# Sample attention with a chunk-free unit at every third turn, and two sets of operands prepared in the same units

## The chip, the cores and the metric

The kernel runs on one core of a Trainium2 chip. The time is that of one execution on the device, in microseconds (us); lower is better. A second, profiled execution of the same program gives the trace.

## What is computed

One layer of a decoder trunk, for a prompt of 512 tokens and for 8 samples of 4 new tokens each (544 columns in all, d_model 2048), float32 throughout:

```
h    = rmsnorm(x) * g_pre
proj = h @ w_in                       # pu, pz, q, kv, ag, az, su, sz, mg
br_pool = (pool_mixer(pu)         * silu(pz)) @ w_br_pool
br_att  = (sparse_attention(q,kv) * silu(az)) @ w_br_nsa
z       = gelu(s5(su))
br_ssm  = (z * sigmoid(z @ w_glu) * silu(sz)) @ w_br_ssm
merged  = sum over branches of sigmoid(mg) * br
y       = x + rmsnorm(merged @ w_out) * g_post
```

The samples attend to 2048 cached positions each, which lie in pages that a page table names: a compressed copy of them, the selected blocks of them, and a window of 512.

## The kernel before

**Units.** TensorE (PE) gets almost all of its work as *units*: a tile of weights of 128 x 1024 numbers against 544 columns. Each float32 matrix is split in a high and a low part of a rounded type, and `mm3` (L154 to L156) multiplies high x high, low x high and high x low. A unit of the input projection (`in_unit`) is 48 such matmuls of 272 columns; a pool unit is 24. There are 218 input units and 4 pool units, then 8 GLU units, 48 branch units, 32 output units. The weights of a unit come by one DMA of 512 KB (`w_load`, L138) into one of three buffers `wr`; ScalarE makes `whi` (L149) and VectorE `wlo` (L150).

**Background work.** Everything else (cache compression, the state-space scan, both attentions, the operands of the next stage) is written as Python generators. `step(u, ...)` emits one unit: it runs what was deferred, lets each generator in `bg` go on to its next `yield`, evicts the unit before (L332, on VectorE), and emits the unit's matmuls. So the number of yields decides beside which unit a piece of background work stands, and each engine works its instructions off in the order in which they were emitted. `main_bg` chains the generators: `g_compress`, `g_ssm`, `g_compress_prompt`, `g_prompt`, `g_decode`, `prep_y(0, ...)`, `prep_z`. With the flag `early` (it is on in `g_compress`, `g_ssm`, `g_decode` and the two preparations) the weights of the unit after next are split and the next load is issued ahead of the background work.

**Compression.** `g_compress` has 16 jobs (8 samples, two halves of a block). A job needs 16 pages of 128 KB, which SyncE's queue (SP) gathers into a tile `ca` of two buffers (L604). A job is three pieces of 20, 20 and 24 matmuls (L638), one unit apart; the gathers for the next job go out with the first and second piece.

**Decode.** `g_decode` walks 20 chunks (4 pairs of samples, 4 chunks of selected positions and one window chunk). Two generators alternate inside it: `s_gen` makes the scores of a chunk from the key tiles `gk` (L1478) and asks for the `gk` two chunks ahead; `p_gen` transposes the weights (L1529), multiplies the chunk before with the value tiles `gv` (L1561) and asks for the `gv` two chunks ahead. Each pass of the loop `while gens` is one turn, and there is one `yield`, so one unit, per turn:

```
        while gens:
            for g in gens[:]:
                try:
                    next(g)
                except StopIteration:
                    gens.remove(g)
            yield
```

`gk` and `gv` have four buffers each, two per chunk. A chunk's gathers are 8 DMAs of 128 KB for `gk` and 8 for `gv`; a window chunk has two DMAs of 512 KB in place of the eight (`wkT`, `wv`). In front of every four gathers SP reads page numbers (`TENSOR_LOAD ptrow`).

**Operands.** `prep_y(0, ...)` loads the pool branch and its gate (`ly`, `lz`), multiplies them (L1628), and splits the product in `yhA` (ScalarE, L1606) and `ylA` (VectorE, L1610), one tile of 128 x 544 per unit. `prep_z` then loads the scan's output in `ly` (L1652, L1654), makes its gelu (square L1644, scale L1645, product L1646, tanh L1647, product L1640), and splits it in `yhB`, `ylB`. The eight GLU units that follow use `yhB`, `ylB`; the first branch uses `yhA`, `ylA`. PSUM has three buffers `d` for the units' sums.

Of the kernel before, what the change touches and what calls it, by code (L numbers as in the profile page):

```python
# [10 lines left out]
F32 = mybir.dt.float32  # L11
F32R = mybir.dt.float32r
I32 = mybir.dt.int32
AF = mybir.ActivationFunctionType
OP = mybir.AluOpType
# [8 lines left out]
TOK = TP + NB * TS  # L24
# [42 lines left out]
def kernel(ctx, tc, a):  # L67
    nc = tc.nc
    pe, dve, act, pool, sp = nc.tensor, nc.vector, nc.scalar, nc.gpsimd, nc.sync
# [25 lines left out]
    ypool = drt("ypool", [8, 128, TOK])  # L95
# [511 lines left out]
    def g_compress():  # L607
        with ExitStack() as s:
            cp = s.enter_context(R("cmp"))
            wphi = cp.tile([128, 2, 32, 64], F32, name="wphi")  # L610
            sp.dma_start(wphi, a["wphi"])
            ca_s = ExitStack()
            cap = ca_s.enter_context(R("ca", 2))
            jobs = [(b, h) for b in range(8) for h in range(2)]
            tiles = {}

            def fetch(n, pages):
                if n >= len(jobs):
                    return
                b, h = jobs[n]  # L620
                if n not in tiles:
                    tiles[n] = cap.tile([128, 16, 256], F32, name="ca")
                gather([tiles[n][:, pg, :] for pg in pages], f"c{h}", b * 16 + pages[0])
            for pg in range(0, 16, 4):
                fetch(0, range(pg, pg + 4))
                yield
            acc_b = None
            for n, (b, h) in enumerate(jobs):
                t = tiles.pop(n).rearrange("q g (k e j) -> q g k e j", k=2, j=8)
                if h == 0:  # L630
                    acc_b = bank("s", 2)
                for d0, d1, pgs in ((0, 5, (0, 8)), (5, 10, (8, 16)), (10, 16, ())):
                    if pgs:
                        fetch(n + 1, range(*pgs))
                    for d in range(d0, d1):
                        dd = h * 16 + d
                        for k in range(2):
                            pe.matmul(acc_b[k * 64:(k + 1) * 64, :128], lhsT=wphi[:, k, dd, :],  # L638
                                      rhs=t[:, :, k, d, :], start=(dd == 0), stop=(dd == 31))
                    yield  # L640
                if h:
                    act.activation(KC[:, b, :], acc_b[:, :128], AF.Copy)
            yield
            ca_s.close()
        done.add("cache")
# [677 lines left out]
    def g_decode():  # L1323
# [239 lines left out]
            next_of(vpos, get_v)  # L1563

        gens = [p_gen(), s_gen()]
        while gens:
            for g in gens[:]:
                try:
                    next(g)
# [3 lines that stand above are left out]
# [20 lines left out]
    YH, YL = {}, {}  # L1593
# [20 lines left out]
    def prep_y(br, src, sil):  # L1614
        YH[br], YL[br] = [], []
        yz, fins = {}, []
        for k in range(10):
            if k < 8:
                y = yps["ld"].tile([128, TOK], F32, name="ly", bufs=3)
                z = yps["ld"].tile([128, TOK], F32, name="lz")  # L1620
                sp.dma_start(y, src[k])
                sp.dma_start(z, zsil[sil][k])
                yz[k] = (y, z)
            if fins:
                fins.pop()()
            if 0 < k < 9:
                y, z = yz.pop(k - 1)
                dve.tensor_tensor(y, y, z, op=OP.mult)  # L1628
                fins.append(split_y(br, y, 0.5))
            yield  # L1630

    def prep_z():
        YH["z"], YL["z"] = [], []
        yz, mid, fins = {}, [], []
        for k in range(11):
            if fins:
                fins.pop()()
            if mid:
                y, z = mid.pop()
                dve.scalar_tensor_tensor(y, z, 1.0, y, op0=OP.add, op1=OP.mult)  # L1640
                fins.append(split_y("z", y, 0.5))
            if 0 < k < 9:
                y, z = yz.pop(k - 1)
                act.activation(z, y, AF.Square)  # L1644
                dve.tensor_scalar(z, z, 0.044715, 1.0, op0=OP.mult, op1=OP.add)  # L1645
                dve.tensor_tensor(z, z, y, op=OP.mult)  # L1646
                act.activation(z, z, AF.Tanh, scale=0.7978845608028654)  # L1647
                mid.append((y, z))
            if k < 8:
                y = yps["ld"].tile([128, TOK], F32, name="ly", bufs=3)  # L1650
                z = yps["ld"].tile([128, TOK], F32, name="lz")
                sp.dma_start(y[:, :512].rearrange("q (l m) -> q l m", l=8),  # L1652
                             y_p[:, 2 * k:2 * k + 2].rearrange("l c g m -> (c g) l m"))
                sp.dma_start(y[:, 512:].rearrange("q (t b) -> q t b", t=4),  # L1654
                             y_s[:, 2 * k:2 * k + 2].rearrange("l c g b -> (c g) l b"))
                yz[k] = (y, z)
            yield


# [12 lines left out]
    def main_bg():  # L1672
        early[0] = True
        yield from g_compress()
        yield from g_ssm()
        early[0] = False
        yield from g_compress_prompt()
        yield from g_prompt()
        early[0] = True
        yield from g_decode()  # L1680
        att_s.close()
        open_y()
        yield from prep_y(0, ypool, "pz")
        yield from prep_z()

    first_tiles()
    u = 0
# [58 lines left out]
    def br_unit(u, b, m):  # L1746
# [10 lines left out]
        def evac():  # L1757
            g = gt.pop((b, m))
            if b == FIRST:
                o = acc_p.tile([128, TOK], F32, name="acc")  # L1760
            else:
                o = g
            for hf in range(2):
                c = slice(hf * HALF, (hf + 1) * HALF)
                dve.scalar_tensor_tensor(o[:, c], g[:, c], 1.0, ps2[hf][:, :HALF], op0=OP.add, op1=OP.mult)
            if b == FIRST:
                ACC[m] = o
            elif b != LAST:
                pool.tensor_tensor(ACC[m], ACC[m], o, op=OP.add)
            else:  # L1770
                dve.tensor_tensor(o, ACC.pop(m), o, op=OP.add)
                h = yps["B"].tile([128, TOK], F32R, name="mh", tag=("yhB", "ylB")[m // 8])
                l = acc_p.tile([128, TOK], F32R, name="ml", tag="acc")
                act.activation(h, o, AF.Copy, scale=0.5)
                dve.scalar_tensor_tensor(l, o, 0.5, h.bitcast(F32), op0=OP.mult, op1=OP.subtract)
                if m == 0:
                    MS.append(yps["ld"].tile([128, 16, 32], F32, name="lz"))
                act.activation(MS[0][:, m], o[:, TP:], AF.Copy, scale=0.5)
                MH[m], ML[m] = h, l
        step(u, mms, evac)  # L1780
# [400 lines left out]
```

## Time and profile before

| what | value |
|---|---|
| median of 3 runs | 2268.2 us (2267.27 to 2268.97) |
| the profiled execution's own time | 2266.38 us |
| its span, first to last instruction | 2264.5 us |
| mean granted TensorE clock | 0.997 |
| PE busy | 2238.5 us, 99% |
| weight loads of PE | 2110.6 us, 93% |
| VectorE, ScalarE, GpSimd busy | 1091.3, 643.9, 119.1 us |
| moved by DMA | 359.60 MB, 159 GB/s |

Read it so: the span is the time between the first and the last instruction of the profiled execution; 1.9 us of its own time lie around it. Matmuls are pipelined, and a matmul that the trace shows as 0.29 us long is followed by the next after 0.125 us; PE busy means that one was under way, not that it ran at its best pace. The granted clock is a share of 2.4 GHz; 0.50 is 1.2 GHz.

### The profile page before, as it was taken

What the parts mean: (1) busy time and instruction counts of PE and PEld (TensorE: products, weight loads), DVE (VectorE), ACT (ScalarE), POOL (GpSimd) and SP (SyncE); (2) the same over time, 40 slices, a digit from 0 to 9 for tenths busy, and PEclk for the clock granted to TensorE, in tenths of its full rate; (3) what the DMA queues carried; (4) which work ended last, traced back from release to release, by engine and by line L of the source; (5) the groups of instructions that cost most, each with busy time, mean ns of one, the idle gap of its engine ahead of it and who ended that gap; (6) DMA issues with size and microseconds to landing.
All of it is one profiled execution on the core that took longest, in us unless ns stands there. A gap on an engine that the chain in (4) does not pass through costs nothing.

```text
span 2264.5 us, 46954 instructions
## 1 busy us (share of the span) xinstructions
PE 2238.5 (99%) x19510; PEld 2110.6 (93%) x19510; DVE 1091.3 (48%) x1999; ACT 643.9 (28%) x1110; POOL 119.1 (5%) x101
## 2 busy tenths in 40 slices
PE   9999999999999999999999999999999999999998
PEld 8899999999999999999999998779999999998778
DVE  6334553347863236766666334332455536453224
ACT  5111111132122114445444323222343212222221
POOL 2000000230052000000000000000000002100000
PEclk9999999999999999999999999999999999999999
DMA  6767776643346765223222468884554645343334
GB/s 228 196 174 195 203 225 197 146 123 106 110 124 144 206 209 169 86 91 116 92 90 77 135 206 248 262 264 153 196 136 141 216 153 203 129 142 107 101 101 153
DMA packets 290791, 359.60 MB, mean 159 GB/s; under 512 B 136338, under 2 KB 210835, under 8 KB 289555
## 3 DMA queue, kind: packets, MB, share of 16 engines
q1 hardware_dynamic: 290578, 356.60, 51.7%
q8 instruction: 154, 2.52, 0.5%
q14 instruction: 59, 0.48, 0.1%
HBM read 310.69 MB, written 54.13 MB: 161 GB/s over the span
## 4 chain that ended last, share of the span: by engine, by line
PE 96%; DMA 2%; SPq 1%; DVE 0%; issue 0%; ACT 0%; ACTq 0%
PE d L154 25%; PE d L156 24%; PE d L155 24%; PE s L638 3%; PE o L1281 2%; PE s L1217 2%; PE t L1257 2%; PE d L1861 2%; PE d L1862 1%; PE d L1863 1%; PE t L1861 1%; PE s L999 1%; PE t L1862 1%; PE t L1863 1%; PE s L1478 1%; PE o L1561 1%
## 5 line engine op out<-in xcount | busy, mean ns | idle before, releaser
L154 PE MATMUL d<-xh,whi 128*128 128x272 f32 x3424 | 1008.0, 294 | 5.5 <-ACT xh L239 5.5
L156 PE MATMUL d<-xl,whi 128*128 128x272 f32 x3424 | 986.4, 288 | 0.0
L155 PE MATMUL d<-xh,wlo 128*128 128x272 f32 x3424 | 985.2, 288 | 0.0
L154 PEld LDWEIGHTS d<-xh,whi 128*128 128x128 f32 x3424 | 646.4, 189 | 31.4 <-issue 20.6
L156 PEld LDWEIGHTS d<-xl,whi 128*128 128x128 f32 x3424 | 646.3, 189 | 1.0 <-DVE xl L240 1.0
L155 PEld LDWEIGHTS d<-xh,wlo 128*128 128x128 f32 x3424 | 646.6, 189 | 0.0
L150 DVE TENSOR_TENSOR wlo<-wr,whi 128x1024 fp32r<-128x1024 f32 x297 | 377.2, 1272 | 510.3 <-ACT whi L149 488.3
L149 ACT ACTIVATE whi<-wr 128x1024 fp32r<-128x1024 f32 x297 | 311.6, 1052 | 739.9 <-PE d L156 485.5
L332 DVE TENSOR_TENSOR e<-d,rstd 128x272 f32<-128x272 f32 x186 | 81.5, 438 | 248.3 <-PE d L156 235.1
L154 PE MATMUL d<-yhA,whi 128*128 128x272 f32 x512 | 148.0, 289 | 0.0
L156 PE MATMUL d<-ylA,whi 128*128 128x272 f32 x512 | 147.7, 288 | 0.0
L155 PE MATMUL d<-yhA,wlo 128*128 128x272 f32 x512 | 147.3, 288 | 0.0
L156 PE MATMUL d<-ylB,whi 128*128 128x272 f32 (+2 forms) x384 | 110.8, 289 | 0.0
L154 PE MATMUL d<-yhB,whi 128*128 128x272 f32 (+2 forms) x384 | 110.8, 289 | 0.0
L155 PE MATMUL d<-yhB,wlo 128*128 128x272 f32 (+2 forms) x384 | 110.4, 287 | 0.0
L154 PEld LDWEIGHTS d<-yhA,whi 128*128 128x128 f32 x512 | 96.3, 188 | 0.0
L155 PEld LDWEIGHTS d<-yhA,wlo 128*128 128x128 f32 x512 | 96.3, 188 | 0.0
L156 PEld LDWEIGHTS d<-ylA,whi 128*128 128x128 f32 x512 | 96.2, 188 | 0.0
L1236 ACT ACTIVATE pt<-s,mm 128x512 f32<-128x512 f32 (+3 forms) x128 | 66.7, 530 | 36.8 <-DVE mm L1232 36.1
L638 PE MATMUL s<-ca,wphi 128*64 128x128 f32 x1024 | 67.6, 280 | 5.8 <-DMA ca<-c 5.8
L155 PEld LDWEIGHTS d<-yhB,wlo 128*128 128x128 f32 x384 | 72.3, 188 | 0.0
L154 PEld LDWEIGHTS d<-yhB,whi 128*128 128x128 f32 x384 | 72.2, 188 | 0.0
(428 smaller groups left out, 2531.2 us busy)
## 6 DMA issues: line engine op xcount, KB each, us to landing
wr<-wd SPq DMA_DIRECT2D x297, 512.0 KB, 3.8
ca<-c SPq DMA_DIRECT2D x256, 128.0 KB, 3.7
gk<-ck SPq DMA_DIRECT2D x128, 128.0 KB, 3.1
gv<-cv SPq DMA_DIRECT2D x128, 128.0 KB, 3.0
gates<-e SPq DMA_DIRECT2D x48, 272.0 KB, 3.9
lg<-gates SPq DMA_DIRECT2D x48, 272.0 KB, 4.0
wo<-wd SPq DMA_DIRECT2D x12, 512.0 KB, 3.5
wphi<-wphi SPq DMA_DIRECT2D x2, 2048.0 KB, 10.7
```

The source lines that it names most:

```text
L149: act.activation(hi, r, AF.Copy)
L150: lo_eng[0].tensor_tensor(lo, r, hi.bitcast(F32), op=OP.subtract)
L154: pe.matmul(ps, lhsT=h, rhs=xh, start=start, stop=False)
L155: pe.matmul(ps, lhsT=l, rhs=xh, start=False, stop=False)
L156: pe.matmul(ps, lhsT=h, rhs=xl, start=False, stop=stop)
L332: dve.tensor_tensor(out[:, cols(hf)], ps[:, :HALF], rstd[:, cols(hf)], op=OP.mult)
L638: pe.matmul(acc_b[k * 64:(k + 1) * 64, :128], lhsT=wphi[:, k, dd, :], rhs=t[:, :, k, d, :], start=(dd == 0), stop=(dd == 31))
L1217: pe.matmul(st[n][k][:, off:off + nk], lhsT=QS[pg][k][:, qt * 128:(qt + 1) * 128], rhs=KS[br, k][j][:, :nk], start=(j == 0), stop=(j == 1))
L1236: act.activation(pt[:, off:off + nk], b[:, off:off + nk], AF.Exp, scale=0.125, bias=m_[:, k, j:j + 1], accum_out=s_[:, k, j:j + 1])
L1257: pe.transpose(b[:, c:c + 128], st[n][k][:, c:c + 128], ident)
L1281: pe.matmul(o[hs[k], qt * 128:(qt + 1) * 128], lhsT=VN[:, kb, br, pg // 4, hs[k]], rhs=st[n][k][:, off + kb * 128:off + (kb + 1) * 128], s ...
L1861: pe.matmul(ps[:, :w], lhsT=MH[k][:, c], rhs=h[:, j], start=(k == 0), stop=False)
```

## The change

```
@@ g_compress
             for pg in range(0, 16, 4):
                 fetch(0, range(pg, pg + 4))
                 yield
+            yield
             acc_b = None
@@ g_decode
         gens = [p_gen(), s_gen()]
+        turn = 0
         while gens:
+            turn += 1
+            if turn > 3 and turn % 3 == 1:
+                yield
             for g in gens[:]:
@@ prep_y
-                z = yps["ld"].tile([128, TOK], F32, name="lz")
+                z = yps["ld"].tile([128, TOK], F32, name="lz", bufs=3)
@@ prep_z becomes prep_first
-    def prep_z():
-        YH["z"], YL["z"] = [], []
-        yz, mid, fins = {}, [], []
+    def prep_first():
+        for br in (0, "z"):
+            YH[br], YL[br] = [], []
+        ld, mid_, fin0 = {}, [], []
         for k in range(11):
-            if fins:
-                fins.pop()()
-            if mid:
-                y, z = mid.pop()
+            if fin0:
+                fin0.pop()()
+            finz = None
+            if mid_:
+                y, z = mid_.pop()
                 dve.scalar_tensor_tensor(y, z, 1.0, y, op0=OP.add, op1=OP.mult)
-                fins.append(split_y("z", y, 0.5))
-            if 0 < k < 9:
-                y, z = yz.pop(k - 1)
-                act.activation(z, y, AF.Square)
-                dve.tensor_scalar(z, z, 0.044715, 1.0, op0=OP.mult, op1=OP.add)
-                dve.tensor_tensor(z, z, y, op=OP.mult)
+                finz = split_y("z", y, 0.5)
+            now = ld.pop(k - 1, None)
+            if now:
+                y0, z, y = now
+                dve.tensor_tensor(y0, y0, z, op=OP.mult)
+                fin0.append(split_y(0, y0, 0.5))
+                act.activation(z, y, AF.Square, scale=0.21146071)
+            if finz:
+                finz()
+            if now:
+                dve.scalar_tensor_tensor(z, z, 1.0, y, op0=OP.add, op1=OP.mult)
                 act.activation(z, z, AF.Tanh, scale=0.7978845608028654)
-                mid.append((y, z))
+                mid_.append((y, z))
             if k < 8:
-                y = yps["ld"].tile([128, TOK], F32, name="ly", bufs=3)
-                z = yps["ld"].tile([128, TOK], F32, name="lz")
+                y0, z, y = (yps["ld"].tile([128, TOK], F32, name=n, bufs=3)
+                            for n in ("ly", "lz", ("ly", "lz")[k % 2]))
+                sp.dma_start(y0, ypool[k])
+                sp.dma_start(z, zsil["pz"][k])
                 sp.dma_start(y[:, :512]..., y_p[...])
                 sp.dma_start(y[:, 512:]..., y_s[...])
-                yz[k] = (y, z)
+                ld[k] = (y0, z, y)
             yield
@@ main_bg
-        yield from prep_y(0, ypool, "pz")
-        yield from prep_z()
+        yield from prep_first()
```

`g_compress` waits one unit more between its last gather for the first job and the first matmul. In the decode, every third turn from the fourth on has a unit without a chunk ahead of it. The two preparations become one: each step takes a tile of the first branch and a tile of the gelu, and one operation on VectorE fewer (the factor 0.044715 goes into the square). The buffers `lz` become three everywhere.

On SP's queue at the start of the compression, the first rows before are the last of the first job's gathers; then comes a weight load, then the gathers for the second job.

```order
L604 DMA ca<-c 128x256
L138 DMA wr<-wd 128x1024
L600 TENSOR_LOAD ptrow
L604 ISA
L604 DMA ca<-c 128x256
```

In the changed kernel the same place reads:

```order
L604 DMA ca<-c 128x256
L138 DMA wr<-wd 128x1024
L460 DMA u_p<-e_903 128x8x64
L462 DMA u_s<-e_903 128x4x8
L138 DMA wr<-wd 128x1024
L600 TENSOR_LOAD ptrow
L604 ISA
L604 DMA ca<-c 128x256
```

The second job's gathers have moved behind one more unit's weight load and behind the stores of one evicted tile.

On SP's queue in the decode, at the end of a turn with two sets of gathers, the rows before are the last gather of `gk`, a store of gates, one weight load, and the next turn's gathers for `gv`.

```order
L604 DMA gk<-ck 128x256
L440 DMA gates<-e_17466 128x544
L138 DMA wr<-wd 128x1024
L600 TENSOR_LOAD ptrow
L604 ISA
L604 DMA gv<-cv 128x256
```

In the changed kernel, at a turn with a free unit ahead of it:

```order
L604 DMA gk<-ck 128x256
L440 DMA gates<-e_17460 128x544
L138 DMA wr<-wd 128x1024 x2
L600 TENSOR_LOAD ptrow
L604 ISA
L604 DMA gv<-cv 128x256
```

Between the two turns' gathers there are now two weight loads, the second of which belongs to the free unit's step. The loop over the chunks has 26 units with chunks in both kernels, and 8 without in the changed one.

On VectorE in the preparation, one step of the gelu before is the weights' low part, the low part of the tile before, the product, the scale, the product, and the eviction.

```order
L150 TENSOR_TENSOR wlo<-wr,whi 128x1024
L1610 SCALAR_TENSOR_TENSOR ylB<-ly,yhB 128x544
L1640 SCALAR_TENSOR_TENSOR ly<-lz,ly 128x544
L1645 TENSOR_SCALAR lz<-lz 128x544
L1646 TENSOR_TENSOR lz<-lz,ly 128x544
L332 TENSOR_TENSOR e_20002<-d,rstd 128x272
```

In the changed kernel one step is:

```order
L150 TENSOR_TENSOR wlo<-wr,whi 128x1024
L1615 SCALAR_TENSOR_TENSOR ylA<-ly,yhA 128x544
L1648 SCALAR_TENSOR_TENSOR ly<-lz,ly 128x544
L1653 TENSOR_TENSOR ly<-ly,lz 128x544
L1615 SCALAR_TENSOR_TENSOR ylB<-ly,yhB 128x544
L1659 SCALAR_TENSOR_TENSOR lz<-lz 128x544
L332 TENSOR_TENSOR e_20130<-d,rstd 128x272
```

A step of the first branch (low part `ylA`, product L1653) has joined the step of the gelu, and the scale has gone. The eviction stands behind five operations of the preparation in place of four.

## Rows read from the trace of the kernel before

**Rows 1.** The page's first part: busy us, share of the span, instructions.

```profile
PE 2238.5 (99%) x19510; PEld 2110.6 (93%) x19510; DVE 1091.3 (48%) x1999; ACT 643.9 (28%) x1110; POOL 119.1 (5%) x101
```

**Rows 2.** Waits of PE in the whole span: us, times, longest.

```profile
PE s L1478 <- DMA gk<-ck: 6.3, 6, 1.9
PE s L638 <- DMA ca<-c: 5.8, 2, 3.9
PE s L1478 <- DMA gk<-wkT: 1.1, 1, 1.1
```

**Rows 3.** Timeline of PE, then windows: us, busy of engines, clock, DMA share, GB/s.

```profile
78.75 1.12 PE L638 MATMUL s<-ca,wphi 128*64 128x128 f32 x8 [3.93 <-DMA ca<-c]
...
78.75:88.79 10.04, 10.04 (x69) 9.56 (x69) 0.00 (x0) 0.00 (x0) 0.00 (x0) 0.71 0.94 269
103.91:111.34 7.43, 7.43 (x69) 7.11 (x68) 1.84 (x2) 1.06 (x1) 0.00 (x0) 1.00 0.26 77
...
78.75:84.00 5.25, 5.25 (x33) 4.92 (x34) 0.00 (x0) 0.00 (x0) 0.00 (x0) 0.50 1.00 270
```

**Rows 4.** Windows of the decode, cut at starts of turns.

```profile
1380.98:1415.58 34.60, 34.60 (x388) 30.34 (x387) 13.31 (x19) 9.91 (x14) 0.00 (x0) 1.00 0.84 261
1415.58:1424.71 9.13, 9.13 (x111) 7.88 (x110) 2.91 (x6) 2.54 (x5) 0.00 (x0) 1.00 0.68 202
1424.71:1477.02 52.31, 48.21 (x496) 39.57 (x495) 16.61 (x27) 12.98 (x20) 0.00 (x0) 0.97 0.83 263
1477.02:1519.29 42.27, 38.80 (x387) 30.83 (x386) 13.45 (x19) 10.75 (x16) 0.00 (x0) 1.00 0.87 280
1439.26:1443.00 3.74, 3.74 (x13) 2.31 (x14) 0.00 (x0) 0.00 (x0) 0.00 (x0) 0.54 0.88 262
```

**Rows 5.** Timeline of SP's queue in the decode: start, us, issues.

```profile
1467.15 4.38 SPq L604 DMA_DIRECT2D gv<-cv  x8
1472.13 5.55 SPq L604 DMA_DIRECT2D gk<-ck  x8
1477.79 0.38 SPq L138 DMA_DIRECT2D wr<-wd  x1
1478.76 4.73 SPq L604 DMA_DIRECT2D gv<-cv  x8
```

**Rows 6.** A window with units alone on PE.

```profile
1600.00:1640.00 40.00, 40.00 (x321) 40.00 (x321) 19.41 (x27) 11.61 (x15) 0.00 (x0) 1.00 0.56 195
```

**Rows 7.** The pool unit's wait: timeline of SP, window.

```profile
202.40 6.90 SPq L604 DMA_DIRECT2D ca<-c  x8
...
210.58:212.45 1.87, 0.00 (x0) 0.03 (x1) 1.83 (x5) 0.00 (x0) 0.00 (x0) 1.00 1.00 237
```

**Rows 8.** DMA from 1400 to 1520: totals, issues to landing.

```profile
DMA packets 23950, 32.32 MB, mean 269 GB/s; under 512 B 2663, under 2 KB 20095, under 8 KB 23935
...
gk<-ck SPq DMA_DIRECT2D x64, 128.0 KB, 2.8
...
gv<-wv SPq DMA_DIRECT2D x6, 512.0 KB, 8.3
```

**Rows 9.** Timeline of VectorE in prep_z and after it.

```profile
1654.87 1.23 DVE L150 TENSOR_TENSOR wlo<-wr,whi 128x1024 fp32r<-128x1024 f32 x1 [3.60 <-ACT whi L149]
...
1695.77 1.23 DVE L150 TENSOR_TENSOR wlo<-wr,whi 128x1024 fp32r<-128x1024 f32 x1 [1.32 <-ACT whi L149]
...
1697.55 0.72 DVE L1640 SCALAR_TENSOR_TENSOR ly<-lz,ly 128x544 f32<-128x544 f32 x1
1699.54 0.45 DVE L1645 TENSOR_SCALAR lz<-lz 128x544 f32<-128x544 f32 x1 [1.27 <-ACT lz L1644]
...
1700.66 0.43 DVE L332 TENSOR_TENSOR e<-d,rstd 128x272 f32<-128x272 f32 x1
...
1716.82 0.44 DVE L332 TENSOR_TENSOR e<-d,rstd 128x272 f32<-128x272 f32 x1 [4.18 <-PE d L156]
```

**Rows 10.** DMA from 1640 to 1710: issues to landing.

```profile
ly<-y_p SPq DMA_DIRECT2D x8, 256.0 KB, 4.1
```

More of the change, by code (lines that the diff above doesn't have):

```diff
@@ L1776, in evac @@
                 if m == 0:
-                    MS.append(yps["ld"].tile([128, 16, 32], F32, name="lz"))
+                    MS.append(yps["ld"].tile([128, 16, 32], F32, name="lz", bufs=3))
                 act.activation(MS[0][:, m], o[:, TP:], AF.Copy, scale=0.5)
```

## The prediction

> **What bounds the kernel now.** I read the page first. Its first part gives TensorE (PE) 2238.5 us of busy time in a span of 2264.5 us [rows 1], so at most 26 us of the span is PE idle, and only what changes PE's own stretch can move the end. The list of waits then says where PE waits for something named [rows 2]: 6.3 + 1.1 = 7.4 us for the decode's key tiles `gk`, and 5.8 us for the tiles `ca` of the compression. The rest of the 26 us is the kernel's start and its tail, which the change does not touch.
>
> The list is too small in one respect: it holds only time in which PE stood still. So I read the two places by windows whose ends are the starts of equal pieces of work.
>
> *Start of the compression.* The first matmul of L638 starts at 78.75, 3.93 us after PE ran dry, because the last pages of the first `ca` tile landed then [rows 3]. From 78.75 to 88.79 PE does one piece of 20 matmuls of L638 and one unit; it takes 10.04 us, while the same piece and unit at 103.91 take 7.43. The granted clock says why: 0.50 from 78.75 to 84.00, which is 1.2 GHz instead of 2.4. The place costs 3.93 + 2.61 = 6.5 us, not 3.9.
>
> *The decode.* A turn is one chunk of scores, one of transposes and products, and one unit. The job repeats every five turns. Four turns and then the fifth take 34.60 and 9.13 us while nothing is late, 43.73 together; the next five take 52.31, and the four after them 42.27 [rows 4]. That is 52.31 - 43.73 = 8.58 and 42.27 - 34.60 = 7.67 us more, 16.2 us in all, of which PE stood still for 7.4 by the list. Part of the rest is the clock again (0.54 from 1439.26 to 1443.00).
>
> Why are the `gk` late? The queue of SP shows it [rows 5]. Eight page gathers take 4.38 us to issue where SP waits for nothing, up to 5.55 here; one turn with 8 gathers for `gv`, 8 for `gk` and a weight load lasts from 1467.15 to 1478.76, 11.61 us. A turn of PE lasts 43.73/5 = 8.75. Three of every five turns are such full ones; in the other two a window load (two DMAs) replaces one set of gathers, and SP catches up. It falls behind PE by up to 2.9 us in each full turn.
>
> **The change, part by part.**
>
> *One unit more before the first chunk of the compression.* The first L638 then has one unit more ahead of it: 48 matmuls at 321 in 40 us [rows 6], 5.98 us. The data came 3.93 us late, and the gathers for the first tile stay at their place in SP's queue while the next tile's eight move behind them by a unit, so they do not come later. Margin 2.0 us: PE does not stop, and the clock has no cause to fall. Term: -6.5 us. Bounds: 0 (the data comes as late again) to -6.5.
>
> *The same shift at the pool units.* The whole compression moves one unit against the pool units, which are half as long (24 matmuls). Before, one of the four fell on the second piece of a job, when the second half of the next tile is fetched, and there PE waited 1.87 us with the clock at 1.00 [rows 7], so a wait of that length costs no more than itself. Shifted by one, the first and the fourth fall there. Bounds: -1.9 (no wait) to +1.9 (two waits). I take 0: SP needed 6.90 us for that half, against 4.38 for eight gathers in the decode, and the two new places need not repeat that.
>
> *A free unit at every third turn.* The built order has 26 turns with chunks before and after, and 8 units without a chunk among them. In a free unit SP has a weight load, 0.38 us and some 0.2 of pauses, while PE works 5.98 us. Per five turns PE then offers 43.73 + 5/3 x 5.98 = 53.7 us. SP's need at its loaded pace is what the late five turns took, 52.3, plus 5/3 x 0.6 = 53.3; where SP waits for nothing a set takes 4.38 and not 5.55, and it needs less. Both fit, the first by only 0.4. Within three full turns in a row the lag grows to 3 x 2.9 = 8.7. A `gk` is asked for two chunks ahead: two turns and, in such a group, mostly a free unit, 2 x 8.75 + 5.98 = 23.5 us. The lag before the third turn (5.8), the turn itself (11.6) and the landing (2.8) [rows 8] make 20.2. So I expect nearly all of the 16.2 back, and leave 3 for the thin margin. Term: -13.2; bounds -16.2 (all) and -8 (half of it stays).
>
> The free units cost PE nothing: it runs the same units and chunks, in another order, and the 8 units are taken from the ones that stood without chunks behind the decode.
>
> The Trainium skill, DMA: Bandwidth & Descriptors, section "Issuing engines are not separate DMA queues", says that the sequencer's time to start a transfer is usually small relative to the transfer. By that the bytes would bind here and not SP; 4.38 us for eight gathers against 2.8 for one to land does not agree. What it would give is the first rival.
>
> *The operands of the first branch and of the GLU side by side.* Before, `prep_y` and `prep_z` take 10 + 11 steps; `prep_first` takes 11, of which the last does nothing. With 1 + 8 units later and 10 fewer, it ends one unit earlier than before, so no operand is late for the first GLU unit by the order. What could be late is VectorE and ScalarE: the work per unit rises. In `prep_z` both already run behind PE: six steps, from one `wlo` to another, take 1695.77 - 1654.87 = 40.90 us, 6.82 each, against a unit of 5.98 [rows 9]. A step is a chain from engine to engine (`whi`, `wlo`, low part, product, copy, square, scale, product, tanh). In the changed order it is `whi`, `wlo`, low part, product, product, copy, square, product, tanh: a product (0.72) in place of the scale (0.45), 7.09 us. The lag before: three evictions stand between the one at 1700.66 and the one at 1716.82, which waited for PE; so the former belongs to the unit that ended at 1716.8 - 4 x 5.98 = 1692.9, and is 7.8 us late. Eight longer steps make that 7.8 + 8 x 0.27 = 10.0. PE waits only when an eviction is more than two units late (three PSUM tiles `d`), 12.0 us. Term: 0, with 2.0 us to spare. Lower bound 0, as PE has nothing to gain there (321 matmuls in 40 us); upper bound from the loads, the third rival: +12.7.
>
> *lz with three buffers; one operation less per GLU tile.* 8 fewer on VectorE, in the chain above. The later `prep_y` calls may load further ahead, with PE already full: 0.
>
> **Sum.** The profiled execution took 2266.4 us, 1.8 below the median of the runs shown. 2266.4 - 6.5 + 0 - 13.2 + 0 = 2246.7; at the median, 2248.5 us, 0.87% less.
>
> **The rivals.** (1) *The bytes bind in the decode.* A turn moves 16 x 128 KB, 512 KB of weights and 136 KB of gates, 2.76 MB; three turns and a free unit 8.95 MB. At the 269 GB/s of the late stretch that is 33.3 us against 3 x 8.75 + 5.98 = 32.2: 1.1 us short, 7 us over six such groups, and with a drop of the clock half of the loss, 8 us. [...] Against: the last of those windows moved 280 GB/s, so 269 is no ceiling, and by that figure 32.0 us suffice. Time 2266.4 - 6.5 - 8.1 + 1.8 = 2253.6. (2) *The free unit does not help*: SP is late for another reason than its own pace, and the 16.2 stay: 2261.7. Against it: the pace by itself, 11.61 against 8.75, explains a lag of the size seen. (3) *The loads of `prep_first` land late.* Four loads go out in one unit. That of y waits until its buffer is free, which is after the low part of the tile before, and the square that needs it stands at the same place one step later; so it has one step, 7.09 us, about 1 to issue its two DMAs and 4.1 to land [rows 10], 2.0 to spare. If it took 8.2, twice that, each of some seven steps would grow by 2.1 us, 14.7 in all, of which 2.0 are free: PE waits 12.7 us, time 2261.2. For it: 8.3 us to landing for `gv<-wv` in the decode [rows 8]. Against: that was with DMA at 0.83 and more; where units stand alone it is at 0.56 [rows 6]. (4) *Slower*: the same place and mechanism with a landing of 10 us: each step grows by 3.9 us, 27.3 in all, 25.3 after what is free, against the 19.7 gained: 2273.8. It decides from a landing of 9.2 us.
>
> **How the numbers follow.** Forecast 0.66, rival 1 0.15, rival 2 0.06, rival 3 0.07, rival 4 0.03, no change at all 0.03. Within 0.2% (about what a measurement of this kernel can tell from no change) means 2263.7 to 2272.7. The first four cases are faster, but rivals 2 and 3 lie within 3 us of that line, so a third of them counts as the same: faster 0.90, same 0.07, slower 0.03. The range: low end 2244, the forecast with nothing left in the decode and a little at the pool units; high end 2258, which takes in rival 1 and some of what late loads may cost.
>
> **What would show each step.** No wait of PE for `ca` near 80 us and the clock at 1.00 from 40 to 120. In the decode, no or one or two waits for `gk` below 1 us each, PE at 40.0 of 40 us and the clock at 1.00, SP free at the end of each free unit; if bytes bind, waits stay at the ends of the groups of three while SP stands waiting for landings. At the pool units, waits for `ca` at one or two of four. In the eleven units of the operands, evictions up to 10 us behind PE and no wait of PE for `wlo` or `e`; waits there, released by `ly` or `lz`, would prove the third rival. The forecast is wrong if the free units leave `gk` late, or if the operands' stretch shows PE idle.

## The result and the profile after

The changed kernel takes 2242.2 us (median of 4 runs, 2241.3 to 2243.5), the kernel before 2268.6 in the same comparison: ratio 0.988, 95% interval 0.9865 to 0.990. It is faster, and by more than the range allowed for (2244 to 2258; forecast 2248.5). The profiled execution took 2242.3 us with a span of 2240.6, 23.9 less than before.

The page's first part, of the kernel after:

```profile
PE 2226.0 (99%) x19510; PEld 2104.9 (94%) x19510; DVE 1090.9 (49%) x1991; ACT 644.7 (29%) x1110; POOL 118.0 (5%) x101
```

Its waits of PE (us, times, longest):

```profile
PE d L154 <- ACT xh L239: 6.1, 3, 4.9
PE s L639 <- DMA ypool<-e: 1.3, 1, 1.3
```

Of [rows 2] nothing is left but one wait of 1.3 us at the compression's line (L639, L638 before); `xh` is the kernel's start. Windows of the kernel after, columns as in [rows 3]:

```profile
74.80:80.80 6.00, 6.00 (x58) 5.85 (x58) 1.85 (x2) 0.29 (x1) 0.00 (x0) 1.00 1.02 308
78.75:84.00 5.25, 5.25 (x53) 4.93 (x52) 0.63 (x1) 0.00 (x0) 0.00 (x0) 1.00 0.92 292
1400.00:1440.00 40.00, 40.00 (x438) 35.89 (x437) 14.64 (x22) 11.95 (x18) 0.00 (x0) 1.00 0.82 269
1440.00:1480.00 40.00, 40.00 (x431) 35.74 (x430) 14.69 (x20) 10.40 (x13) 0.00 (x0) 1.00 0.85 275
1480.00:1520.00 40.00, 40.00 (x411) 36.34 (x411) 12.18 (x21) 9.83 (x16) 0.00 (x0) 1.00 0.80 246
1520.00:1560.00 40.00, 40.00 (x437) 36.81 (x439) 15.20 (x23) 12.50 (x19) 0.00 (x0) 1.00 0.77 259
1281.02:1595.87 314.85, 314.82 (x3171) 290.18 (x3168) 109.02 (x162) 83.20 (x119) 2.12 (x1) 1.00 0.69 224
1640.00:1680.00 40.00, 40.00 (x321) 40.00 (x321) 27.17 (x40) 20.63 (x31) 0.00 (x0) 1.00 0.60 179
```

In these windows PE stands still for 0.03 us at most, and the granted clock is 1.00: at the start of the compression (0.50 before, [rows 3]), all through the decode (the row of 314.85 us; 0.97 and waits before, [rows 4]), and beside the joined operands (the last row).

To see where the 23.9 us came from, take two marks that stand in both kernels: the second group of transpositions in the decode's preparation (L1382, L1383 after) and the transposition of the decode's result (L1577, L1582 after). PE's timeline before:

```profile
1282.66 0.49 PE L1382 MATMUL t<-ident,kc 128*32 128x128 f32 x3
...
1565.96 0.38 PE L1577 MATMUL t<-ident,dpt 128*128 128x128 f32 x2
```

And after, with the first matmul of the compression ahead of them:

```profile
79.95 0.44 PE L639 MATMUL s<-ca,wphi 128*64 128x128 f32 x4
...
1281.02 0.49 PE L1383 MATMUL t<-ident,kc 128*32 128x128 f32 x3
...
1595.87 0.38 PE L1582 MATMUL t<-ident,dpt 128*128 128x128 f32 x2
```

At the first mark the changed kernel has done one unit (5.98 us) more and is yet 1.64 earlier: 7.6 gained. Between the marks it has 8 units more, 47.9 us: 314.85 - 47.9 = 267.0 against 283.3, 16.3 gained. Together 23.9, all of the difference.

The 7.6 divide so. Before, PE ran dry at 78.75 - 3.93 = 74.82 [rows 3]; after, the same unit ends at 79.95 - 5.98 = 73.97. These 0.85 us fell in a stretch in which both kernels run the same instructions: an accident of the one execution (in the other traces with the start of the kernel before, that unit ends between 73.6, e7, and 74.9, e1). Then 3.93 of the wait and 2.61 of the half clock, 6.54. At the pool units the wait is 1.87 - 1.33 = 0.5 shorter. That is 7.9; 0.3 went astray in between. The division is that of one pair of executions. The first mark stands anywhere from 1278.57 (e5) to 1282.66 in the traces of kernels whose compression starts as before, so the 0.85, the 0.5 and the 0.3 are no effects of the change that these traces can show. The 16.3 between the marks is steadier, as the traces under e11 show.

### The profile page after: what moved, and what is told of

Its sections match the earlier page's. It is cut to its first block, busy times and chain, and to the rows that moved or that the text cites. A ratio compares the mean times of both kernels' runs of the same rounds, so it can differ in the third digit from the quotient of the medians.

```text
span 2240.6 us, 46952 instructions
## 1 busy us (share of the span) xinstructions
PE 2226.0 (99%) x19510; PEld 2104.9 (94%) x19510; DVE 1090.9 (49%) x1991; ACT 644.7 (29%) x1110; POOL 118.0 (5%) x101
## 4 chain that ended last, share of the span: by engine, by line
PE 98%; DMA 0%; SPq 0%; DVE 0%; ACT 0%; issue 0%; ACTq 0%
PE d L154 25%; PE d L156 24%; PE d L155 24%; PE s L639 3%; PE o L1282 2%; PE s L1218 2%; PE t L1258 2%; PE d L1875 2%; PE d L1877 1%; PE d L1876 1%; PE o L1562 1%; PE t L1875 1%; PE s L1000 1%; PE t L1877 1%; PE s L1479 1%; PE t L1876 1%
## 5 line engine op out<-in xcount | busy, mean ns | idle before, releaser
L156 PEld LDWEIGHTS d<-ylB,whi 128*128 128x128 f32 x384 | 72.3, 188 | 0.0
```

Source lines behind the costliest of these rows:

```text
L156: pe.matmul(ps, lhsT=h, rhs=xl, start=False, stop=stop)
```

## The experiments

All ratios are to the kernel before in the same comparison; its medians there were 2266.0 (e1 to e4), 2262.6 (e5 to e7), 2267.1 (e8 to e11) and 2265.9 (e12 to e14). Where a run is set against the changed kernel of another comparison, the difference holds to about 1 us: the changed kernel took 2242.2 in the first comparison and 2243.1 in that of e11.

**Undoing one part at a time (e1, e2), and the third part alone (e3).** e1 takes this line out of the changed kernel, in `g_compress`:

```
                 yield
-            yield
             acc_b = None
```

> The changed kernel without the extra unit before the first chunk of the compression; free units and joined operands stay. Theory (each part gives what the trace of before shows as lost at its place, and the parts do not touch each other): the wait for the first ca tile of some 3.9 us and the half clock behind it come back, 6.5 us, and the pool unit's 1.87 in place of 1.33: 2242.2 + 7.0 = 2249.2 us. Rival A (what is lost at the start of the compression is made up later): within 2 us of 2242.2. Rival B (the unit shifts everything behind it, and part of the decode's gain hangs on that): above 2252.

Measured 2248.6 us (2245.4 to 2250.1), 0.992 [0.991, 0.993]: 6.4 more than the changed kernel. The wait is back:

```profile
78.58 1.76 PE L638 MATMUL s<-ca,wphi 128*64 128x128 f32 x14 [3.69 <-DMA wr<-wd]
```

The list names a weight load here and `ca` in the kernel before; the matmul reads `ca`, whose last page goes out at 74.06 and lands 4.2 us later. Neither rival holds.

e2 takes out the free units:

```
-            if turn > 3 and turn % 3 == 1:
-                yield
```

> The changed kernel without the free units in the decode; the extra unit of the compression and the joined operands stay. Theory: the late gk come back with all their 16.2 us, so the profiled execution takes 2242.3 + 16.2 = 2258.5; and since the waits for gk are what differs from run to run, the runs scatter as those of before do and their median lies 1 to 3 us above the profiled execution, 2259.5 to 2261.5. Rival A (the gap of 2 us between median and profile comes from elsewhere, the start of the compression above all): median within 0.5 us of the profile. Rival B (the free units also help something outside the decode): over 2263.

Measured 2258.5 us (2256.3 to 2262.7), 0.997 [0.996, 0.998]: 16.3 more than the changed kernel. The waits of PE in this kernel show `gk` again:

```profile
PE s L1479 <- DMA gk<-ck: 5.6, 5, 1.4
PE s L1479 <- DMA gk<-wkT: 0.6, 2, 0.4
```

As in the kernel before, the list names less than half of what the place costs; where the rest lies is shown under e5. Median and profile (2257.3) differ by 1.2, between the theory and rival A; the seven runs spread over 6.4 us, those of the changed kernel over 2.3.

e3 is the kernel before with `prep_first` and three `lz` buffers alone.

> The kernel before with the joined preparation of operands and three lz buffers alone. Theory: no time, within 1 us of the 2268.6 of before. Rival (the remainder of 1 to 3 us that the other two parts do not explain comes from the operands: fewer operations, fewer steps behind the decode): 2265.5 to 2267.5.

Measured 2266.7 us, 1.000 [0.999, 1.001]: no time, as the theory has it. The bounds in us on record were counted from 2268.6; in this comparison the kernel before took 2266.0, so that 2266.7 lies within the rival's figures without the gain that the rival stands for.

**How many free units (e4).** `turn % 3 == 1` becomes `turn % 4 == 1`.

> The changed kernel with a free unit ahead of every fourth turn in place of every third. Theory (SP's queue needs 53.0 us for five turns, PE would offer 43.73 + 5/4 x 5.98 = 51.2): SP falls 1.8 us behind per five turns, and late gk with short waits come back in the second half of the decode: 3 to 8 us lost of the 16.2, 2245 to 2250. Rival A (any free unit suffices, since the lag of one group of three full turns is what counts): 2242 to 2243.5. Rival B (the place of the free units against the window chunks decides, and a fourth turn misses the full ones): 2252 or more.

Measured 2247.1 us (2245.7 to 2247.7): 4 to 5 of the 16.3 are lost again (against 2243.1 of e11 and 2242.2), with single waits of 1.4 and 1.3 us for `gk`. That is the size that SP's pace gives; both rivals fall. (e4 has six free units, the changed kernel eight.)

**Is it SP's queue or the bytes? (e5, e6, e7).** All three are the kernel before with one thing changed in the decode's gathers. e5:

```
-                    gather([t[:, pg] ... for pg in range(4)], "cv", b_ * 16 + c * 4)
+                    sp.dma_start(t, a["cv"].rearrange(...)[:, b_ * 16 + c * 4:b_ * 16 + c * 4 + 4])
```

> The kernel before; in the decode each tile of four pages comes by one DMA of 512 KB from a fixed place in place of four DMAs of 128 KB at pages read from the page table (the page table is left out there; bytes and rows of 1 KB stay). Theory (SP's time to issue makes the gk late): a turn's 11.6 us on SP's queue fall to about 3, no gk is late, the 16.2 us come back: 16 below the kernel before, 2250 to 2252. Rival (the bytes bind): 2.76 MB a turn need 10.3 us at 269 GB/s against a turn of 8.75, the gk stay late and the time is within 3 us of the kernel before.

Measured 2248.0 us (2246.5 to 2249.8), 0.994 [0.992, 0.995], 14.7 below the kernel before (16 forecast). SP's queue in e5:

```profile
1456.96 0.92 SPq L1351 DMA_DIRECT2D gv<-cv  x2
1458.31 0.92 SPq L1341 DMA_DIRECT2D gk<-ck  x2
```

The same 16 pages of 128 KB that took 4.38 + 5.55 = 9.9 us to issue [rows 5] take 1.8, no `gk` is late, and the stretch from 1400 to 1520 moves 286 GB/s; so 269 [rows 8] was no ceiling. e5 also leaves out the reading of page numbers, so it shows that SP's time is the limit and not which part of that time.

Between the two marks PE works the same list in e5 as in the kernel before, so the two traces show where the loss lies. Windows from mark to mark, before and in e5, and then the same two windows with the matmuls of L1478 alone:

```profile
1282.66:1565.96 283.30, 275.71 (x2786) 244.21 (x2784) 95.53 (x146) 72.69 (x107) 2.14 (x1) 0.99 0.74 233
1278.57:1545.71 267.14, 267.11 (x2787) 242.46 (x2785) 95.54 (x146) 72.69 (x107) 2.15 (x1) 1.00 0.73 247
1282.66:1565.96 283.30, 28.07 (x160) 4.71 (x160) 0.99 0.74 233
1278.57:1545.71 267.14, 21.09 (x160) 3.88 (x160) 1.00 0.73 247
```

Of the 16.2 us, 7.6 are PE standing still (283.30 - 275.71), 7.0 are longer busy time of the same 160 matmuls of L1478 (28.07 - 21.09), and the remaining 1.6 go with the stretch at half clock. The 7.0 look so, in the kernel before and in e5:

```profile
1489.31 1.05 PE L1478 MATMUL s<-gk,qbd 128*32 128x512 f32 x4 [1.02 <-DMA gk<-ck]
1490.96 1.05 PE L1478 MATMUL s<-gk,qbd 128*32 128x512 f32 x4 [0.60 <-DMA gk<-ck]
```

```profile
1491.84 1.04 PE L1478 MATMUL s<-gk,qbd 128*32 128x512 f32 x8
```

A chunk has eight such matmuls, four for each of its two tiles `gk`. With both tiles there, all eight take 1.04 us; with one coming after the other, each four take as long. This part stands in no list of waits. In e2 it is there too (28.48 us of L1479), with the clock at 1.00 throughout.

e6 leaves the gathers as they are and gives those for `gv` to GpSimd's queue:

```
-            sp.dma_start(dst, a[table]...)
+            (q or sp).dma_start(dst, a[table]...)
...
-                    gather([t[:, pg] for pg in range(4)], "cv", b_ * 16 + c * 4)
+                    gather([t[:, pg] for pg in range(4)], "cv", b_ * 16 + c * 4, pool)
```

> The kernel before with the gathers for gv issued by GpSimd's queue; those for gk and the weights stay on SP's. Bytes and the number of gathers stay. Theory: SP's full turn falls from 11.6 to about 6 us, below PE's 8.75, and gk is on time: 16 below the kernel before, 2250 to 2252. Rival A (the bytes bind): within 3 us of before. Rival B (GpSimd issues slower than SP, and gv becomes the late tile): up to some 10 below before, or above it, with waits of PE for gv in the trace.

Measured 2248.2 us (2244.4 to 2248.7), 0.993 [0.992, 0.995], 14.4 below. There is no wait for `gk` or `gv`. GpSimd in e6 (four gathers in 2.29 us, then the reading of page numbers):

```profile
1457.64 2.29 POOL L604 DMA_DIRECT2D gv<-cv  x4 [3.48 <-PE o L1561]
1460.45 2.29 POOL L604 DMA_DIRECT2D gv<-cv  x4 [0.52 <-issue]
1466.67 2.29 POOL L604 DMA_DIRECT2D gv<-cv  x4 [3.93 <-PE o L1561]
```

It waits for PE to free a buffer before each set of eight: the queue is ahead of PE. The same edit with ScalarE's queue:

> The kernel before with the gathers for gv issued by ScalarE's queue. Theory: SP is as free as with GpSimd's queue, and gk on time; ScalarE pays some 4.4 us of issuing per turn beside some 3 us of busy time per turn, below 8.75, so it should hold: 2250 to 2253. Rival A (the bytes bind): within 3 us of before. Rival B (whi and the exponentials queue behind the gathers on ScalarE): waits of PE for whi or for the transposed weights, 2256 or more.

Measured 2281.3 us, 1.009 [1.007, 1.010]: slower. The waits of PE in this kernel:

```profile
PE s L1478 <- ACT S L1495: 10.2, 2, 5.4
PE t L1529 <- ACT dpt L1543: 6.3, 2, 3.7
```

ScalarE's timeline in it:

```profile
1447.42 6.73 ACTq L604 DMA_DIRECT2D gv<-cv  x8
1454.19 1.06 ACT L149 ACTIVATE whi<-wr 128x1024 fp32r<-128x1024 f32 x1 [8.76 <-DMA gv<-cv]
```

Rival B, and worse than it said. ScalarE's share of time had room, but `whi`, the copies of a window chunk's scores (`S`, L1495) and the copies `dpt` stand in its queue behind the gathers, and PE waits for the last two.

e7 halves each gather (`dst` and the page cut to half of their columns, a `pool.memset` for the rest).

> The kernel before; each gather of the decode brings half a page, 64 KB, and GpSimd fills the other half with zeros (half of the keys and values are left out). As many DMAs from SP's queue, half of their bytes. Theory (SP's time to issue binds, 4.38 us for eight): the gk stay late, 10 to 16 of the 16.2 us remain, 0 to 6 below the kernel before. Rival (the bytes bind): a turn moves 1.7 MB, 6.3 us at 269 GB/s, and all of the 16.2 come back: 2250 to 2252.

Measured 2260.5 us, 0.9987 [0.998, 0.9996]: 2.2 below, so most of the loss stays although the decode moves 199 GB/s in place of 269. SP's queue in e7:

```profile
1473.45 4.74 SPq L604 DMA_DIRECT2D gv<-cv  x8
1478.79 4.63 SPq L604 DMA_DIRECT2D gk<-ck  x8
...
1485.25 4.39 SPq L604 DMA_DIRECT2D gv<-cv  x8
```

Eight gathers of 64 KB take 4.39 us to issue where SP waits for nothing, eight of 128 KB 4.38 [rows 5]. Rival 1 of the prediction, the bytes, is excluded: halving those of the gathers leaves most of the loss, and e5 and e6 move all of them without it.

The Trainium skill, DMA: Bandwidth & Descriptors, section "Issuing engines are not separate DMA queues", says that the sequencer's time to start a transfer is usually small relative to the transfer. For one gather the trace agrees: 4.38 / 8 = 0.55 us to issue, 2.8 to land [rows 8]; the prediction had set eight issues against one landing. What binds here is the sum of sixteen issues on one queue.

One thing stays open. SP's pace in the late turns is not issuing alone. Its own waits between 1400 and 1520 in the kernel before begin so:

```profile
SPq L604 <- DMA gv<-wv: 4.7, 6, 0.9
SPq L604 <- DMA wr<-wd: 3.3, 4, 1.7
```

By this list gathers wait for loads of 512 KB that were issued ahead of them; in e7, which leaves those loads as they were, the same two lines read 4.7 and 2.3 us. Single gathers also take longer than the others: among the eight that took 5.55 us in [rows 5] one takes 1.51 us and the other seven 0.33 each, and the trace names no reason. Without it that turn would have lasted 10.4 us, still above PE's 8.75, so issuing alone is enough to fall behind; how much of the 16.3 the rest adds was not tried.

**The margin beside the operands (e8).** In the changed kernel VectorE works so:

```profile
1638.92 1.23 DVE L150 TENSOR_TENSOR wlo<-wr,whi 128x1024 fp32r<-128x1024 f32 x1 [1.87 <-ACT whi L149]
...
1674.04 1.22 DVE L150 TENSOR_TENSOR wlo<-wr,whi 128x1024 fp32r<-128x1024 f32 x1 [1.32 <-ACT whi L149]
...
1677.90 0.43 DVE L332 TENSOR_TENSOR e<-d,rstd 128x272 f32<-128x272 f32 x1
...
1686.61 0.44 DVE L332 TENSOR_TENSOR e<-d,rstd 128x272 f32<-128x272 f32 x1 [0.60 <-PE d L156]
```

Five steps in 35.12 us are 7.02 each (predicted 7.09). The eviction at 1686.61 waited for PE; two stand between it and the one at 1677.90, which belongs to the unit that ended three units earlier, at 1668.6: 9.3 us late (predicted 10.0). e8 doubles two operations:

```
         def fin():
             dve.scalar_tensor_tensor(l, y, scale, h.bitcast(F32), ...)
+            if br in (0, "z"):
+                dve.scalar_tensor_tensor(l, y, scale, h.bitcast(F32), ...)
```

> The changed kernel with each low part of the joined preparation computed twice, two operations of 0.64 us more per step on VectorE. In the changed kernel a step takes 7.02 us and VectorE ends 9.3 us behind PE. Theory (a step is a chain that no engine overlaps, and PE waits from a lag of 12.0 us, three buffers d): the step becomes 8.30, eight of them make the lag 9.3 + 8 x 1.28 = 19.5, and PE waits 7.5 us: 2249.7 us. Rival A (the chain has slack that takes the operations up, or PE waits only much later): within 1.5 us of 2242.2. Rival B (PE waits from a lag of less than 10 us, as the weights' low parts are late before the evictions are): 2252 or more.

Measured 2249.3 us (2248.7 to 2249.9), 6.2 above the changed kernel of the same comparison (e11). The waits of PE in e8:

```profile
PE d L154 <- DVE e L332: 4.5, 3, 2.0
```

Both rivals fall. The wait is for `e`, the eviction, as the limit of three buffers `d` says. Its size, 6.2 us of time against 7.5 forecast, fits a limit of 12 to 13 us. So the changed kernel runs some 3 us inside that limit, by this estimate.

**What the joined operands are for (e13).** The changed kernel with `prep_y(0, ...)` and `prep_z` in place of `prep_first`:

```
-        yield from prep_first()
+        yield from prep_y(0, ypool, "pz")
+        yield from prep_z()
```

> The changed kernel with the operands prepared as before, one set after the other (21 steps in place of 11); the extra unit and the free units stay. Theory (the joined preparation takes no time and saves none, but it makes room for the nine units that the other two parts put ahead of it): the last 6 or 7 steps find no unit of the input projection left to stand beside and run with PE idle, some 6 us each: 36 to 45 us more than the changed kernel, 2278 to 2287. Rival (the preparation had room behind it, and the steps still end in time): 2242 to 2244.

Measured 2264.3 us (2263.5 to 2266.7), 0.9993 [0.998, 1.000]: 21 us more than e12 of the same comparison, and all but nothing is left of the gain. The theory's kind is right, its size nearly twice too large. A window and the waits of PE in e13:

```profile
1680.00:1720.00 40.00, 26.06 (x153) 22.83 (x152) 25.30 (x39) 18.90 (x30) 0.00 (x0) 0.74 0.41 101
```

```profile
PE d L156 <- DVE ylB L1615: 8.5, 5, 1.9
...
PE d L154 <- ACT yhB L1611: 5.4, 6, 1.1
```

PE's timeline there:

```profile
1701.77 0.58 PE L154 MATMUL d<-yhB,whi 128*128 128x256 f32 x1 [0.92 <-ACT yhB L1611]
1704.18 0.58 PE L156 MATMUL d<-ylB,whi 128*128 128x256 f32 x1 [1.62 <-DVE ylB L1615]
1705.68 0.58 PE L154 MATMUL d<-yhB,whi 128*128 128x256 f32 x1 [0.92 <-ACT yhB L1611]
```

The GLU's first unit takes its operands tile by tile. It waits for each of the last ones, made every 3.9 us (1705.68 - 1701.77) and not every 6, and does its share of work in between, at a clock of 0.74.

**The first part alone (e14).** The kernel before with the one `yield` in `g_compress`.

> The kernel before with the extra unit ahead of the first chunk of the compression alone. Theory: 6.5 us less than before, from the wait of 3.9 and the half clock behind it; the preparation ends one unit later, and there is room for one. Rival A (the wait moves to another place of the compression): within 2 us of before. Rival B (no room at the end of the operands): one step without a unit beside it, so some 6 us are given back, within 1 us of before.

Measured 2258.9 us (2256.9 to 2263.4), 0.996 [0.995, 0.998]: 7.1 below, so the first term stands by itself and there was room for one unit more behind the operands. The wait at the pool units (`ypool<-e`) is 1.9 us here.

**The wait at the pool units (e9, e10, e12).** e9 adds a queue to the changed kernel's gathers, as e6 does, for `ca`:

```
-                gather([tiles[n][:, pg, :] for pg in pages], f"c{h}", b * 16 + pages[0])
+                gather([tiles[n][:, pg, :] for pg in pages], f"c{h}", b * 16 + pages[0], pool if pages[0] == 8 else None)
```

> The changed kernel with the second half of each ca tile (from the second job on) gathered by GpSimd's queue instead of SP's. Theory (the one wait at a pool unit, 1.33 us, is SP's time to issue eight gathers again): the wait goes, 2241 us. Rival (it waits for a store to finish, whatever queue gathers): 2242.2 and the wait stays. The two lie near what five rounds resolve; the trace of waits decides.

Measured 2244.5 us (2243.5 to 2245.4): no better. The wait at L639 has gone, but there is another:

```profile
PE d L155 <- DVE wlo L150: 1.6, 1, 1.6
```

That wait stands at 64.76 us, at the kernel's start: the condition also moved four gathers of the first job, where the text on record said that it spared them. e10 puts the queue in the place of the free units:

> The kernel of the run before this one (second half of ca on GpSimd's queue), without the free units, and with the gathers for gv on GpSimd's queue in their place. Theory (the free units do nothing but give SP time): the same time as with the free units, within 1 us, 2241. Rival (the free units also help by less contention between chunks, or the queue's descriptors cost something): 2243.5 or more.

Measured 2244.4 us, the same as e9: what the free units do, a second queue does too, and nothing more. e12 spares the first job (`pool if n and pages[0] == 8 else None`):

> The changed kernel with the second half of each ca tile from the second job on gathered by GpSimd's queue; the first job's gathers stay on SP's, where the run before moved four of them too and PE waited 1.6 us for wlo near 65 us. Theory (that wait came from the four gathers that went out beside the stores of u at the start): neither that wait nor the one for ca at a pool unit, 1.0 to 1.5 below the changed kernel, 2241 to 2242. Rival (GpSimd's queue costs something all along the compression): 2243.5 or more again.

Measured 2243.2 us (2242.9 to 2244.6), between the theory's and the rival's. The wait at L639 is gone, 0.7 us of the one for `wlo` stays, and the time is that of the changed kernel (2242.2 and 2243.1). There is nothing to be had here that these runs can measure. No kernel tried is faster than the changed one.

**The changed kernel again (e11).**

> The changed kernel unaltered, timed again. So far the kernel before gave medians of 2268.6, 2266.0 and 2262.6 in three comparisons, and the kernels whose gk are on time 2248.6, 2248.0 and 2248.2 (all with the late start of the compression). Theory (what varies from chip to chip is the loss at late gk, not the rest): the changed kernel gives 2242.2 +- 0.8 again, whatever the kernel before gives. Rival (chips differ by a factor for every kernel): it keeps its ratio of 0.988 to the kernel before of the same comparison.

Measured 2243.1 us (2241.4 to 2244.0), 0.990 [0.988, 0.991]. That is 0.9 above the theory's 2242.2, just outside its bound, and 2.8 above the rival's 2267.1 x 0.9882 = 2240.3. The theory is nearer, but with the kernel before so close to its first median the run does not settle it.

The traces say more. Take the stretch between the two marks of the decode and subtract 5.98 us for each free unit. The changed kernel takes 267.0 us there, and so do e8, e9, e11, e12 and e13, which run the same instructions in it, all within 0.1 us (e1 0.5 more). e5, e6 (GpSimd) and e10 take 267.1, 267.2 and 266.9: whatever cures the late `gk`, the same time is left. Where `gk` is late, the same instructions take 282.4 (e2), 283.3 (the kernel before), 284.7 (e3) and 286.1 us (e14). So the loss itself is what varies in this stretch, from 15.4 to 19.1 us.

## Why the prediction was right and wrong

The mechanisms held; two sizes did not, that of the free units and the step from the profile to the median, and the rest is scatter. 2248.5 - 2242.2 = 6.3 us are to be explained.

- **The first unit: right.** -6.5 forecast; 6.54 in the trace, 6.4 (e1) and 7.1 (e14) by removing and by adding it. How close is in part luck: from 77 to 85 us the mean granted clock was 0.57 in the kernel before and 0.79 in e5, e6 (GpSimd) and e7, which have a wait of 3 to 4 us at the same place, so its share of the term differs from one execution to the next.
- **The pool units: 0 forecast, 0.5 shorter in this pair.** One of the two new places waited (1.33 us), the other did not. But the wait differs between executions: with the compression as before it is 1.87, 1.7 (e1), 0.8 (e3) and none (e5, e7), with the extra unit 1.33, 1.9 (e14), 0.7 (e4), 0.6 (e8) and 0.3 (e11). No gain is shown, and 0 was right as far as these traces tell.
- **The free units: the step that failed.** The prediction costed the loss at 16.2 us, found that SP would fit by 0.4 us per five turns, and then wrote "leave 3 for the thin margin". Nothing was left: 16.3 between the marks and in e2. So the term was -16.3 where the prediction had -13.2, and the low end of its range took for an extreme what was the plain case. The margin was not wider than thought. Three full turns in a row take 12.48, 11.04 and 12.27 us on SP's queue, from one set of `gv` to the next, no less than the 11.61 of before:

```profile
1424.95 4.39 SPq L604 DMA_DIRECT2D gv<-cv  x8
...
1437.43 4.38 SPq L604 DMA_DIRECT2D gv<-cv  x8
...
1448.47 4.38 SPq L604 DMA_DIRECT2D gv<-cv  x8
...
1460.74 6.77 SPq L604 DMA_DIRECT2D gv<-cv  x8
1467.62 1.02 SPq L1344 DMA_DIRECT2D gk<-wkT  x2
...
1474.44 1.04 PE L1479 MATMUL s<-gk,qbd 128*32 128x512 f32 x8
```

  The second `gk` of the last two rows goes out at 1468.26 and lands 5.4 us later, 0.75 us before the first matmul of its chunk (0.3 in e11); no other chunk has less. But a tile that lands in time costs nothing, however little in time it is. The balance had come out as fitting, and the 3 us stood for no wait that it had found. The model itself was good: with one free unit fewer in four (e4) it gave 3 to 8 us lost, and 4 to 5 were.
- **From the profile to the median: wrong, 1.8.** Before, the profiled execution was 1.8 us below the median of the runs, and the prediction carried this over. After, both are 2242.3 and 2242.2. In the later comparisons the kernel before ran from 2259 to 2272 us, with medians from 2262.6 to 2267.1, so 1.8 was scatter. Kernels with late `gk` spread widely within a comparison (e2 6.4 us, e14 6.5), those with the late first `ca` alone less (e5 3.2, e6 with GpSimd 4.4, e1 4.7), the changed kernel and e8 least (2.3, 2.5 in e11, 1.2). That the scatter goes with the stalls fits these numbers and the stretches under e11; it was not tried by itself.
- **An accident, 0.85.** The start of the kernel ran faster in the one profiled execution.
- **The operands: right.** Term 0, no wait; 7.02 us a step and 9.3 us of lag against 7.09 and 10.0, and e8 found the limit near where it was put. What the prediction did not price is that without this part the nine units ahead of it cost 21 us (e13).

What is off adds up to 3.1 (decode) + 0.5 + 1.8 + 0.85, less the 0.3 that went astray, 5.95 of the 6.3; the rest is rounding and the time around the span. Of these only the decode's 3.1 is a wrong cost. The low end of the range allowed for the first two only.

Of the rivals, the first falls by e5 to e7 (what the prediction held against it, eight issues against one landing, compares unlike things, as said under e7), the second by e2, the third and fourth because no load of `prep_first` was waited for.

## What to carry to other kernels

Cost a late transfer by windows between equal marks, not by the list of waits: here 7.4 us of named waits stood for 16.3, and most of the rest was matmuls of the same line that ran one group after another and counted as busy. When a queue of issues is the limit (eight gathers 4.4 us, at 64 KB as at 128), fewer and larger DMAs, an idle engine's queue, or work without gathers between the bursts all gave the same 14 to 16 us here; an engine that computes for the same loop was the wrong place for them here (e6 with ScalarE). If a sum of terms fits with the whole loss recovered, forecast that, put the doubt into the range, and don't carry one execution's distance from the median to a kernel without the stalls.

## What the runs showed of the hardware

- The time to issue a gather did not depend on its bytes: eight take 4.39 us at 64 KB (e7) and 4.38 at 128 KB [rows 5], while two DMAs of 512 KB take 0.92 (e5). Of the 0.55 us for one gather, 0.33 are its own instruction (the median for `gk`, before and in e7 alike); the rest is reading page numbers and setting addresses. Nor did it depend on how busy the DMA engines were: in the kernel before the median is 0.33 us where their share of the 3 us ahead of the issue was below 0.5, and where it was above 0.95.
- GpSimd's queue issues such gathers at SP's pace, four in 2.29 us (e6), and the profile counts this as busy time of GpSimd (189.3 us in e6, 119.1 before).
- Matmuls of 32 columns that wait for a late tile cost more than the wait: four take 1.05 us where eight together take 1.04 (e5), and the profile shows no wait for the difference.
- A stretch of 120 us of the decode moved 286 GB/s in e5 and e6, 17 above the 269 of [rows 8], without a late tile.
